# Gates of the linear recurrence: two products of 64 rows with both gates' columns, in place of two block-diagonal products of 128 rows

## The chip, the cores and the metric

The kernel runs on one core of one Trainium2 chip. A core has five engines with queues of their own: PE (TensorE, the matrix products; its weight loads are counted apart as PEld), DVE (VectorE), ACT (ScalarE), POOL (GpSimd) and SP (SyncE, which mainly issues DMAs). The time is that of one execution on the device in microseconds; the number that counts is the median of several executions.

## The reference, cut to what matters

One layer of a decoder trunk is computed for 2048 prompt tokens and 8 sample tokens. Each token's normed row goes through one input projection; a part of its columns feeds a retention block, another part a linear recurrence (RG-LRU), and both go through an output projection, a norm and a gated feed-forward part. The change touches the recurrence. Its 512 channels are 8 blocks of 64, and each block has two gates, `r` and `i`, with a 64x64 matrix each:

```python
xc, s_conv_lru_new = causal_dwconv(x_lru, s_conv_lru, conv_lru_w, conv_lru_b)
...
xb = x32.reshape(B, T, N_LRU_BLOCKS, LRU_BLOCK)
r = jax.nn.sigmoid(jnp.einsum('btnd,nde->btne', xb, w_r).reshape(B, T, W) + b_r)
i = jax.nn.sigmoid(jnp.einsum('btnd,nde->btne', xb, w_i).reshape(B, T, W) + b_i)
log_a = -LRU_C * r * jax.nn.softplus(-lam)
a = jnp.exp(log_a)
mult = jnp.sqrt(-jnp.expm1(2.0 * log_a))
...
bterm = mult * i * x32
# h[t] = a[t] * h[t-1] + bterm[t]
lru_out = hl * jax.nn.gelu(g_lru)
```

All inputs and outputs are 32-bit floats.

## The kernel before, in words

Channels lie on the 128 partitions and tokens run along the free dimension. The 2056 tokens are worked in three groups (0 to 2), one after the other; each group has two blocks of 336 to 344 tokens. The large products (input projection, output projection, feed-forward) are taken as three products in the type fp32r, of high and low parts, by the helper `mm3` (lines 371 to 375); a projection of one weight tile for one block (`proj`) is 8 times `mm3`, that is 24 products of 128x128 with up to 344 columns, into one of the three PSUM banks of the pool `pm`. Nearly everything that PE does is such products.

The recurrence's 512 channels are four tiles `t` of 128, two blocks of 64 in each. For one tile and one token block (24 such pairs in all) three pieces of code work:

- `lru_x` projects the tile's input. ACT copies the result from PSUM twice (lines 785 and 786: `xl`, and `xc` with the first term of the convolution), and the generator `lru_chain` is appended to the list `soon`.
- `lru_chain` adds three more terms of the convolution to `xc` on DVE (line 807), then yields. When it is resumed it takes two plain f32 products, `zr` and `zi` (lines 816 and 817), each with a 128x128 matrix that holds the tile's two 64x64 blocks on its diagonal and zeros elsewhere (`wri`, zeroed by POOL at line 241 and filled by four DMAs at line 246). One such f32 product stands in the trace as two matmul records. ACT evaluates `tanh` of both gates from PSUM (820, 822) and once more for the first gate (821); DVE, ACT and POOL make the decay, the gated input and the scan (823 to 834).
- `lru_g` projects the gate branch of the same tile and block, waits in the program's order until the chain is through (`while g.lru[t, b] is None: advance(soon)`), then ACT takes its GeLU from PSUM into `xc` (line 800) and DVE multiplies by the scan (801); `fsplit` (457, 458) splits the result into high and low parts `mlh` and `mll` for the output projection.

What sets the order: the program is traced item by item, and after each item of rate 1 `advance(soon)` resumes the first generator of `soon` up to its next yield (and goes on to the next generator if that one ends). For one tile `t` the items are `lru_x` of the first and second block, then `lru_g` of the first and second block. So a block's chain runs its convolution after its own `lru_x` or with the end of the other block's chain, and its products one item later. The order on each engine is then settled when the kernel is built: a scheduler simulates the program with a cost model and, among what is ready in that simulation, takes the earlier traced first. The queues then hold the instructions in the order that results. In each group, the items of tile 0 are followed by a head of the retention block (8 projections) and the first part of the output projection, those of tile 1 by another head and another part, and tiles 2 and 3 come one after the other, followed by the last head and the last parts.

PSUM: the pool `pm` has three banks (projections, output and down projections, some of the feed-forward's); the pool `pt` has five (`zr`, `zi`, the retention's tiles and others).

Of the kernel before, what the change touches and what calls it, by code (L numbers as in the profile page):

```python
# [13 lines left out]
AF = mybir.ActivationFunctionType  # L14
ALU = mybir.AluOpType

P = 128
# [81 lines left out]
def hybrid_step(ctx: ExitStack, tc: tile.TileContext, I, O):  # L99
    nc = tc.nc  # L100
    V, S, G, T = nc.vector, nc.scalar, nc.gpsimd, nc.tensor
# [12 lines left out]
    def ctile(cols, name, dt=F32):  # L114
        return con.tile([P, cols], dt, tag=name, name=name)

    def ttile(name):
        return tp.tile([P, BMAX + 4], F32, tag="t", name=name)
# [4 lines left out]
    def pst(name):  # L123
        return pt.tile([P, 512], F32, tag="t", name=name)
# [71 lines left out]
    clb, b_r, b_i = (vec[:, 64 + 4 * i:68 + 4 * i] for i in range(3))  # L196
# [10 lines left out]
    sp2, hbr, hbi = lc[:, 0:4], lc[:, 4:8], lc[:, 8:12]  # L207

    def lru_constants():
        V.tensor_scalar(out=hbr, in0=b_r, scalar1=0.5, scalar2=None, op0=ALU.mult)  # L210
        V.tensor_scalar(out=hbi, in0=b_i, scalar1=0.5, scalar2=None, op0=ALU.mult)
        y_ = tiny(4, "sp_y")
        V.tensor_scalar(out=y_, in0=lam, scalar1=-1.0, scalar2=None, op0=ALU.mult)
        V.tensor_tensor(out=y_, in0=y_, in1=lam, op=ALU.max)
        t_ = tiny(4, "sp_t")
        S.activation(out=t_, in_=y_, func=AF.Tanh, scale=1.0 / 32.0)
        d_ = tiny(4, "sp_d")
        V.tensor_scalar(out=d_, in0=t_, scalar1=1.0, scalar2=None, op0=ALU.add)
        V.reciprocal(d_, d_)
        V.tensor_scalar(out=t_, in0=t_, scalar1=-1.0, scalar2=1.0, op0=ALU.mult, op1=ALU.add)  # L220
        V.tensor_tensor(out=t_, in0=t_, in1=d_, op=ALU.mult)
        for _ in range(4):
            V.tensor_tensor(out=t_, in0=t_, in1=t_, op=ALU.mult)

        V.tensor_scalar(out=d_, in0=t_, scalar1=2.0, scalar2=None, op0=ALU.add)
        V.reciprocal(d_, d_)
        V.tensor_tensor(out=t_, in0=t_, in1=d_, op=ALU.mult)
        w2_ = tiny(4, "sp_w")
        V.tensor_tensor(out=w2_, in0=t_, in1=t_, op=ALU.mult)
        V.memset(d_, 1.0 / 17.0)  # L230
        for n in (15, 13, 11, 9, 7, 5, 3, 1):
            V.tensor_tensor(out=d_, in0=d_, in1=w2_, op=ALU.mult)
            V.tensor_scalar(out=d_, in0=d_, scalar1=1.0 / n, scalar2=None, op0=ALU.add)
        V.tensor_tensor(out=d_, in0=d_, in1=t_, op=ALU.mult)
        V.tensor_scalar(out=y_, in0=lam, scalar1=-1.0, scalar2=0.0, op0=ALU.mult, op1=ALU.max)
        V.scalar_tensor_tensor(out=y_, in0=d_, scalar=2.0, in1=y_, op0=ALU.mult, op1=ALU.add)
        V.tensor_scalar(out=sp2, in0=y_, scalar1=2.0, scalar2=None, op0=ALU.mult)


    wri = ctile(8 * P, "wri")  # L240
    G.memset(wri, 0.0)
    wriv = wri.rearrange("p (g t c) -> p g t c", g=2, t=4)
    for gi, nm in enumerate(("w_r", "w_i")):
        src = I[nm][0].rearrange("(t u) d e -> u d t e", u=2)
        for u in range(2):
            nc.gpsimd.dma_start(out=wriv[64 * u:64 * u + 64, gi, :, 64 * u:64 * u + 64], in_=src[u])
    for i in range(1, len(stage)):
        if i % 2:
            two = ttile("rows")
# [91 lines left out]
    def fetch_operand(key, lo_on):  # L341
# [25 lines left out]
        if (i == 1 or i == 2 and kind == "w_up_conv") and nm in ("A11", "A12"):  # L367

            del pr[nm]

    def mm3(out, wh, wl, xh, xl, first, last, more=False):

        T.matmul(out, wh, xh, start=first, stop=False, skip_group_check=more)  # L373
        T.matmul(out, wh, xl, start=False, stop=False, skip_group_check=more)  # L374
        T.matmul(out, wl, xh, start=False, stop=last, skip_group_check=more)  # L375

    ada_ps = {}

# [95 lines left out]
    class Group:  # L474
# [329 lines left out]
        def lru_chain(g, t, b, xl, xc):  # L804
            n, np_ = b[1] - b[0], g.npr(b)
            for j in range(3):
                V.scalar_tensor_tensor(out=xc[:, 0:np_], in0=xl[:, j:j + np_],
                                       scalar=clw[:, j, t:t + 1], in1=xc[:, 0:np_],
                                       op0=ALU.mult, op1=ALU.add)
                if np_ < n:  # L810
                    V.scalar_tensor_tensor(out=xc[:, np_:n], in0=slc[:, :, j, t],
                                           scalar=clw[:, j, t:t + 1], in1=xc[:, np_:n],
                                           op0=ALU.mult, op1=ALU.add)
            yield
            zr, zi = pst("zr"), pst("zi")
            T.matmul(zr[:, 0:n], wriv[:, 0, t, :], xc[:, 0:n], start=True, stop=True)
            T.matmul(zi[:, 0:n], wriv[:, 1, t, :], xc[:, 0:n], start=True, stop=True)
            s_, ti, rec = ttile("s"), ttile("ti")[:, 0:n], xl[:, 0:n]
            hs, s_ = s_, s_[:, 0:n]
            S.activation(out=s_, in_=zr[:, 0:n], func=AF.Tanh, scale=0.5, bias=hbr[:, t:t + 1])  # L820
            S.activation(out=s_, in_=s_, func=AF.Tanh, scale=sp2[:, t:t + 1], bias=sp2[:, t:t + 1])
            S.activation(out=ti, in_=zi[:, 0:n], func=AF.Tanh, scale=0.5, bias=hbi[:, t:t + 1])
            V.tensor_scalar(out=rec, in0=s_, scalar1=1.0, scalar2=None, op0=ALU.add)
            V.reciprocal(rec, rec)
            V.scalar_tensor_tensor(out=ti, in0=ti, scalar=1.0, in1=xc[:, 0:n], op0=ALU.add, op1=ALU.mult)
            S.activation(out=s_, in_=s_, func=AF.Sqrt)
            G.tensor_tensor(out=s_, in0=s_, in1=rec, op=ALU.mult)
            if g.gi == 0 and b[0] == 0:
                V.memset(s_[:, 0:1], 0.5)
            G.tensor_tensor(out=ti, in0=ti, in1=s_, op=ALU.mult)  # L830
            V.tensor_scalar(out=rec, in0=rec, scalar1=2.0, scalar2=-1.0, op0=ALU.mult, op1=ALU.add)
            V.tensor_tensor_scan(out=hs[:, 0:np_], data0=rec[:, 0:np_], data1=ti[:, 0:np_],
                                 initial=o_h[:, t:t + 1], op0=ALU.mult, op1=ALU.add)
            V.tensor_copy(o_h[:, t:t + 1], hs[:, np_ - 1:np_])
            if np_ < n:
                V.tensor_tensor(out=hs[:, np_:n], in0=rec[:, np_:n], in1=slh[:, :, t], op=ALU.mult)
                V.tensor_tensor(out=hs[:, np_:n], in0=hs[:, np_:n], in1=ti[:, np_:n], op=ALU.add)
                V.tensor_copy(o_hs[:, :, t], hs[:, np_:n])
            g.lru[t, b] = (hs[:, 0:n], xc[:, 0:n])
# [504 lines left out]
    for gi, g in enumerate(gs):  # L1344
        its = group_items(g, gs[gi + 1] if gi + 1 < len(gs) else None)
        if gi == 0:
            todo = [(j, k) for j in (2, 4, 3, 5) for k in range(KC)]
            mixed, c = [], 0.0
# [12 lines left out]
    g = gs[0]  # L1361
    xl = g.xload()

    more = [slot("more").rearrange("p a t -> p (a t)") for _ in range(7)]
    rest = [t[:, 2048:4 * TMAX] for t in more]
    more = [t[:, c:c + 1024] for t in more for c in (0, 1024)]
# [86 lines left out]
```

## Time and profile before

| | |
|---|---|
| median of 3 executions | 2462.89 us (2462.57 to 2464.89) |
| the profiled execution | 2463.86 us, of which 2462.1 us from its first to its last instruction |
| mean granted clock of TensorE | 0.988 |
| PE idle within the span | about 102 us |
| f32 gate products | 48, in 96 matmul records |

The profile counts an engine as busy from an instruction's start to its end. PE's instructions are pipelined: a product's recorded duration is longer than the distance to the next one, so what a product costs PE is read from the distances between starts. A line of the list of waits says which engine and line waited for which, then the sum in us, how often, and the longest. A line of the list of instruction groups has, after the count, the busy time and the mean duration in ns, then the idle time of the engine before these instructions and what ended it. In the windows view each row is a stretch of the span with the busy time of each engine, the granted clock and the DMA share.

### The profile page before, as it was taken

Reading aid. Unit: us, or ns where it says so; the run is one execution under the profiler, and the core shown is the slowest. Engines: PE = TensorE matmul, PEld = TensorE weight load, DVE = VectorE, ACT = ScalarE, POOL = GpSimd, SP = SyncE. Lnnn points to the kernel's source line nnn. Section 1 sums busy time; section 2 is a strip of 40 time slices with the busy share of each in tenths; the row PEclk is TensorE's granted clock in tenths of the full one; section 3 lists DMA queues with packets and bytes.
Section 4 is the critical chain, followed back from the end, with each engine's and each line's share of the span. In section 5 each row is a group of like instructions: output and inputs, shape, how many; then the busy total and the mean of one; then the engine's idle time right before and its main releaser. Section 6 shows DMA issues by size and latency. Waiting matters only on the chain.

```text
span 2462.1 us, 40114 instructions
## 1 busy us (share of the span) xinstructions
PE 2359.8 (96%) x15157; PEld 2275.5 (92%) x15157; DVE 1452.9 (59%) x3181; ACT 869.6 (35%) x1964; POOL 716.9 (29%) x739
## 2 busy tenths in 40 slices
PE   5999998999999999999899999999999989999998
PEld 4987797999999999999899999999999989999998
DVE  5646777875766665666754444446667675444444
ACT  4323554544444444243422222243124241222222
POOL 3444440257666743243001010112222210101011
PEclk9999999999999999999999999999999999999999
DMA  9476655878878875343566666666442465666674
GB/s 299 163 261 223 210 172 190 305 276 287 304 285 304 323 251 184 120 157 139 189 222 235 222 238 220 241 213 215 139 130 96 145 231 199 239 220 234 219 252 160
DMA packets 243493, 536.04 MB, mean 218 GB/s; under 512 B 19223, under 2 KB 114055, under 8 KB 243292
## 3 DMA queue, kind: packets, MB, share of 16 engines
q1 hardware_dynamic: 242220, 532.01, 62.6%
q8 instruction: 120, 1.97, 0.3%
q10 hardware_dynamic: 696, 0.91, 0.1%
q0 software_dynamic: 384, 0.56, 0.1%
q14 instruction: 73, 0.60, 0.1%
HBM read 385.10 MB, written 148.42 MB: 217 GB/s over the span
## 4 chain that ended last, share of the span: by engine, by line
PE 53%; DVE 4%; ACT 2%; DMA 1%; issue 1%; POOL 1%; POOLq 0%; SPq 0%; ACTq 0%; DVEq 0%
PE down L374 6%; PE down L373 6%; PE down L375 6%; PE qx L374 4%; PE qx L375 4%; PE qx L373 4%; PE proj L373 3%; PE proj L375 3%; PE proj L374 3%; PE qz L373 2%; PE qz L374 2%; PE qz L375 2%; PE qy L374 1%; PE qy L373 1%; PE qy L375 1%
## 5 line engine op out<-in xcount | busy, mean ns | idle before, releaser
L851 DVE SCALAR_TENSOR_TENSOR x<-down,mod,x 128x344 f32<-128x344 f32 (+2 forms) x624 | 349.0, 569 | 347.0 <-PE down L375 342.3
L373 PE MATMUL proj<-hh,wb 128*128 128x344 f32 (+1 forms) x1152 | 378.5, 329 | 14.3 <-DVE h L580 6.0
L375 PE MATMUL proj<-hh,wb 128*128 128x344 f32 (+1 forms) x1152 | 373.6, 325 | 2.7 <-POOL wb L304 2.5
L374 PE MATMUL proj<-hl,wb 128*128 128x344 f32 (+1 forms) x1152 | 372.5, 323 | 0.0
L458 POOL TENSOR_TENSOR ffl<-cv,ffh 128x344 fp32r<-128x344 f32 (+1 forms) x120 | 124.7, 1046 | 782.0 <-ACT ffh L457 736.7
L374 PE MATMUL qx<-op,wb 128*128 128x344 f32 (+1 forms) x1020 | 325.5, 319 | 2.6 <-DVE op L921 2.6
L373 PE MATMUL qx<-op,wb 128*128 128x344 f32 (+1 forms) x1020 | 324.7, 320 | 1.2 <-ACT op L920 1.2
L375 PE MATMUL qx<-op,wb 128*128 128x344 f32 (+1 forms) x1020 | 324.5, 319 | 0.0
L373 PE MATMUL down<-ffh,wb 128*128 128x344 f32 (+1 forms) x960 | 304.7, 324 | 7.6 <-DVE x L851 7.4
L375 PE MATMUL down<-ffh,wb 128*128 128x344 f32 (+1 forms) x960 | 306.4, 319 | 0.0
L374 PE MATMUL down<-ffl,wb 128*128 128x344 f32 (+1 forms) x960 | 306.3, 319 | 0.0
L304 POOL TENSOR_TENSOR wb<-wr,wb 128x512 fp32r<-128x512 f32 x164 | 223.9, 1376 | 230.7 <-ACT wb L303 222.1
L373 PEld LDWEIGHTS proj<-hh,wb 128*128 128x128 f32 x1152 | 218.4, 190 | 25.9 <-issue 9.5
L375 PEld LDWEIGHTS proj<-hh,wb 128*128 128x128 f32 x1152 | 218.7, 190 | 5.7 <-POOL wb L304 3.9
L374 PEld LDWEIGHTS proj<-hl,wb 128*128 128x128 f32 x1152 | 219.1, 190 | 3.3 <-POOL hl L588 0.9
L1076 DVE SCALAR_TENSOR_TENSOR cv<-u,vec,cv 128x344 f32<-128x344 f32 (+2 forms) x264 | 170.8, 665 | 50.6 <-ACT cv L1056 48.1
L374 PEld LDWEIGHTS qx<-op,wb 128*128 128x128 f32 x1020 | 191.7, 188 | 3.4 <-DVE op L921 3.4
L373 PEld LDWEIGHTS qx<-op,wb 128*128 128x128 f32 x1020 | 191.5, 188 | 2.0 <-ACT op L920 1.8
L373 PEld LDWEIGHTS down<-ffh,wb 128*128 128x128 f32 x960 | 179.3, 188 | 14.3 <-DVE x L851 13.7
L375 PEld LDWEIGHTS qx<-op,wb 128*128 128x128 f32 x1020 | 191.4, 188 | 0.0
L373 PE MATMUL qz<-op,wb 128*128 128x344 f32 (+1 forms) x528 | 169.7, 325 | 14.6 <-ACT op L920 10.7
L375 PEld LDWEIGHTS down<-ffh,wb 128*128 128x128 f32 x960 | 180.6, 188 | 0.0
(314 smaller groups left out, 4952.1 us busy)
## 6 DMA issues: line engine op xcount, KB each, us to landing
wb<-w_down SPq DMA_DIRECT2D x100, 512.0 KB
wb<-w_up_conv_S SPq DMA_DIRECT2D x92, 512.0 KB
wb<-w_up_gate_S SPq DMA_DIRECT2D x92, 512.0 KB
wb<-w_in SPq DMA_DIRECT2D x72, 512.0 KB
wb<-w_up_conv_A SPq DMA_DIRECT2D x69, 512.0 KB
wb<-w_up_gate_A SPq DMA_DIRECT2D x69, 512.0 KB
w_in<-wb SPq DMA_DIRECT2D x48, 512.0 KB
w_up_conv_S<-wb SPq DMA_DIRECT2D x44, 512.0 KB
```

The lines of the kernel that those rows point to most:

```text
L304: lo_on.tensor_tensor(out=w[:, 512:1024], in0=src, in1=w[:, 0:512].bitcast(F32), op=ALU.subtract)
L373: T.matmul(out, wh, xh, start=first, stop=False, skip_group_check=more)
L374: T.matmul(out, wh, xl, start=False, stop=False, skip_group_check=more)
L375: T.matmul(out, wl, xh, start=False, stop=last, skip_group_check=more)
L458: G.tensor_tensor(out=lo[:, 0:n], in0=src, in1=hi[:, 0:n].bitcast(F32), op=ALU.subtract)
L851: V.scalar_tensor_tensor(out=xs, in0=q[:, 0:np_], scalar=modv[:, jg, m, 0:1], in1=xs, op0=ALU.mult, op1=ALU.add)
L1076: V.scalar_tensor_tensor(out=cv[:, 0:np_], in0=u[:, j:j + np_], scalar=cfw[:, j, ft:ft + 1], in1=cv[:, 0:np_], op0=ALU.mult, op1=ALU.add)
```

## The change

The two 64x64 blocks of a tile are no longer put on the diagonal of one 128x128 matrix for each gate. Instead, each half of the partitions has one product: rows 0 to 63 of `xc` against 64x128 weights that hold both gates' columns of that block, and rows 64 to 127 likewise. The columns are placed so that the `r` gate of a block comes out on its own partitions and the `i` gate on the other half. ACT reads each gate in two halves from the two banks (the `i` gate's halves are moved to the other partitions by the same instruction), so there are five ACT instructions on the products where there were three. The bias of the `i` gate is stored with its halves swapped. `wri` has half the size, every element of it is written by the DMAs, and the memset goes.

Further, the chain yields once more before its products, and the two products are bound to come, in PE's queue, after the last `mm3` product traced so far (`tc.issue_after` adds an ordering edge without a semaphore). By the order of items above, the products of a chain are then traced within `lru_g` of the same tile and block, right after its projection.

```diff
-        V.tensor_scalar(out=hbi, in0=b_i, scalar1=0.5, scalar2=None, op0=ALU.mult)
+
+        for u in range(2):
+            V.tensor_scalar(out=hbi[64 * (1 - u):64 * (1 - u) + 64], in0=b_i[64 * u:64 * u + 64], scalar1=0.5,
+                            scalar2=None, op0=ALU.mult)
...
-    wri = ctile(8 * P, "wri")
-    G.memset(wri, 0.0)
-    wriv = wri.rearrange("p (g t c) -> p g t c", g=2, t=4)
+    wri = ctile(4 * P, "wri")
+    wriv = wri.rearrange("p (t c) -> p t c", t=4)
...
-            nc.gpsimd.dma_start(out=wriv[64 * u:64 * u + 64, gi, :, 64 * u:64 * u + 64], in_=src[u])
+            c = 64 * ((u + gi) % 2)
+            nc.gpsimd.dma_start(out=wriv[64 * u:64 * u + 64, :, c:c + 64], in_=src[u])
...
+    last_mm = [None]
...
-        T.matmul(out, wl, xh, start=False, stop=last, skip_group_check=more)
+        last_mm[0] = T.matmul(out, wl, xh, start=False, stop=last, skip_group_check=more)
...
             yield
-            zr, zi = pst("zr"), pst("zi")
-            T.matmul(zr[:, 0:n], wriv[:, 0, t, :], xc[:, 0:n], start=True, stop=True)
-            T.matmul(zi[:, 0:n], wriv[:, 1, t, :], xc[:, 0:n], start=True, stop=True)
+            yield
+
+            zs = [pst("z0"), pst("z1")]
+            halves = [slice(64 * u, 64 * u + 64) for u in range(2)]
+            with tc.issue_after(last_mm[0].ins):
+                for z, hf in zip(zs, halves):
+                    T.matmul(z[:, 0:n], wriv[hf, t, :], xc[hf, 0:n], start=True, stop=True)
...
-            S.activation(out=s_, in_=zr[:, 0:n], func=AF.Tanh, scale=0.5, bias=hbr[:, t:t + 1])
+            for z, hf in zip(zs, halves):
+                S.activation(out=s_[hf], in_=z[hf, 0:n], func=AF.Tanh, scale=0.5, bias=hbr[hf, t:t + 1])
             S.activation(out=s_, in_=s_, func=AF.Tanh, scale=sp2[:, t:t + 1], bias=sp2[:, t:t + 1])
-            S.activation(out=ti, in_=zi[:, 0:n], func=AF.Tanh, scale=0.5, bias=hbi[:, t:t + 1])
+            for z, hf, other in zip(zs, halves, halves[::-1]):
+                S.activation(out=ti[hf], in_=z[other, 0:n], func=AF.Tanh, scale=0.5, bias=hbi[other, t:t + 1])
```

## The prediction

> **What bounds the kernel now.** I read the page first, then the list of PE's waits, then PE's instruction groups.
>
> ```profile
> span 2462.1 us, 40114 instructions
> ...
> PE 2359.8 (96%) x15157; PEld 2275.5 (92%) x15157; DVE 1452.9 (59%) x3181; ACT 869.6 (35%) x1964; POOL 716.9 (29%) x739
> ```
>
> PE is busy for 2359.8 of 2462.1 us; 102 us are idle. So only two things shorten this kernel: fewer microseconds of product on PE, or fewer waits on PE. The other engines have room on average, and matter where PE waits for one of them.
>
> ```profile
> PE zr L816 <- DVE xc L807: 6.2, 3, 2.9
> ...
> PE proj L373 <- DVE rotb L624: 4.6, 3, 1.9
> ```
>
> ```profile
> L373 PE MATMUL down<-mlh,wb 128*128 128x344 f32 (+1 forms) x192 | 62.2, 324 | 0.0
> ...
> L816 PE MATMUL zr<-xc,wri 128*128 128x344 f32 (+1 forms) x48 | 19.3, 484 | 6.2 <-DVE xc L807 6.2
> L817 PE MATMUL zi<-xc,wri 128*128 128x344 f32 (+1 forms) x48 | 18.4, 467 | 0.0
> ```
>
> The reader is to see two costs of the gates: 96 records of product, and three waits of 6.2 us in sum for the convolution (line 807) just before `zr`. The output projection never waits for the recurrence's result `mlh` (0.0 idle), so a later chain has room at its far end.
>
> **The products.** Their cost is read from starts, in a quiet place of the timeline:
>
> ```profile
> 277.86 0.32 PE L373 MATMUL proj<-hh,wb 128*128 128x344 f32 x1
> 278.01 0.32 PE L374 MATMUL proj<-hl,wb 128*128 128x344 f32 x1
> 278.17 0.32 PE L375 MATMUL proj<-hh,wb 128*128 128x344 f32 x1
> 278.33 0.74 PE L816 MATMUL zr<-xc,wri 128*128 128x344 f32 x2
> 278.90 0.74 PE L817 MATMUL zi<-xc,wri 128*128 128x344 f32 x2
> 279.22 0.58 PE L373 MATMUL proj<-hh,wb 128*128 128x344 f32 x1
> 279.64 0.32 PE L374 MATMUL proj<-hl,wb 128*128 128x344 f32 x1
> ```
>
> A projection's product takes 0.157 us from start to start (277.86 to 278.33 hold three). From 278.17 to 279.64 are 1.47 us, with two such products in them; the four f32 records cost 1.47 - 0.31 = 1.156 us, 0.289 each. For 24 chains that is 27.7 us. After the change a chain still has four records of as many columns. They are cheaper only if the two halves of the array work side by side. No row shows two products on different rows. The nearest show products on different columns of the array (shape 128*2, on four separate strips), and what it costs to leave the full shape and come back:
>
> ```profile
> 1716.17 0.31 PE L374 MATMUL proj<-hl,wb 128*128 128x344 f32 x1
> 1716.41 0.48 PE L756 MATMUL os<-vts,sTs 8*128 8x128 f32 x2
> 1716.62 0.27 PE L756 MATMUL os<-vts,sTs 8*128 8x128 f32 x1
> 1716.82 0.29 PE L759 MATMUL os<-sret,qm 128*2 128x128 f32 x4
> ...
> 1716.83 0.61 PE L759 MATMUL os<-sret,qm 128*2 128x128 f32 x15
> 1717.37 0.42 PE L375 MATMUL proj<-hh,wb 128*128 128x344 f32 x1
> 1717.64 0.45 PE L816 MATMUL zr<-xc,wri 128*128 128x344 f32 x1
> ```
>
> Fifteen f32 records of 128 columns (0.107 us each by the rate above, 1.6 in a row) are done in 0.61 us; and four records of 0.27 us stand within 0.29, so they start within 0.02. Products on separate column strips do run together. I take the same for row halves: 2 x 0.289 + 0.01 = 0.59 us for the pair.
>
> Against it stands the change of shape. From line 374 to the 8-row product of line 756 pass 0.24 us, 0.08 more than 0.157. Its second record comes 0.21 later, where 128 columns take 0.107 at the rate above: 0.10 more, a weight load that nothing hides. On the way back the last record starts at 1716.83 + 0.61 - 0.27 = 1717.17 and should end its columns at 1717.28; the projection's product starts at 1717.37, 0.09 late, and the next at +0.27 in place of 0.157, 0.11 late. An excursion costs 0.08 + 0.10 + 0.09 + 0.11, some 0.39 us with the roundings. So a chain takes 0.59 + 0.39 = 0.98 in place of 1.156: **24 x -0.18 = -4.3 us**. Bounds: nothing for the excursion gives 24 x -0.57 = -13.6; halves one after the other give 24 x 0.39 = +9.4; if the two halves' first loads follow each other (0.10 more) it is -1.9. I take -4.3, the sum of the nearest rows.
>
> The Trainium skill, "TensorEngine Tiling (Array Packing)", section Overview, gives up to 2x for a contract dimension of 64 or less; by that alone the streaming would shrink by half, which is the -13.6. The same page, Tiling Modes, says that changing the mode drains TensorE, without a figure; the 0.39 us of the rows is what it takes here, and two thirds of the gain go there.
>
> **The waits before the products.** The windows around the two longest:
>
> ```profile
> 298.64:301.48 2.84, 0.32 (x2) 0.02 (x2) 2.80 (x5) 1.72 (x3) 1.94 (x2) 1.00 0.58 186
> 302.90:306.40 3.50, 3.50 (x12) 2.12 (x10) 2.97 (x5) 2.17 (x6) 1.27 (x1) 0.51 0.89 277
> 1105.61:1108.50 2.89, 0.31 (x3) 0.03 (x1) 2.85 (x7) 0.77 (x3) 1.31 (x2) 1.00 0.34 135
> 1108.50:1111.90 3.40, 3.06 (x7) 2.14 (x8) 3.33 (x5) 2.03 (x5) 2.55 (x2) 0.50 0.41 117
> 266.00:312.00 46.00, 41.27 (x241) 33.33 (x240) 36.15 (x45) 28.72 (x48) 20.91 (x18) 0.96 0.64 193
> ```
>
> In the first and third row PE stands while DVE (third busy column) works without a break. In the second and fourth the granted clock is half: the PE work there, 3.50 and 3.06 us, would take half the time, a loss of 1.7 + 1.5 = 3.2 us. The half clock follows each of the two long waits, so I charge it to them: 6.2 + 3.2 = **9.4 us**. With the change the products stand one projection later, 24 x 0.157 = 3.77 us, and the longest wait was 2.9. These three waits should go: **-9.4**. All lie in the stretch of tiles 2 and 3, where chains follow each other closely.
>
> **What comes in their place.** The chain now ends one item later, so its DVE and ACT work reaches further into the retention head that follows. In such heads PE already waits for DVE's rotation, 4.6 us in three waits (the list above), 1.5 us each. I charge three more, one per group, behind its last chains: **+4.6**. Bounds: nothing, since `mlh` has a head of eight projections (30 us) before it is read; and above, the bank rival below.
>
> ACT has two instructions more per chain:
>
> ```profile
> L826 ACT ACT_TABLE_LOAD x24 | 30.8, 1283 | 0.4
> L800 ACT ACT_TABLE_LOAD x19 | 24.4, 1283 | 1.3 <-DVE s L829 0.9
> L821 ACT ACTIVATE s<-s,lc 128x344 f32<-128x344 f32 (+1 forms) x24 | 16.1, 669 | 0.1
> ...
> L820 ACT ACTIVATE s<-zr,lc 128x344 f32<-128x344 f32 (+1 forms) x24 | 13.0, 542 | 18.1 <-PE zr L816 18.1
> L822 ACT ACTIVATE ti<-zi,lc 128x344 f32<-128x344 f32 (+1 forms) x24 | 13.0, 540 | 1.0 <-PE zi L817 0.6
> L826 ACT ACTIVATE s<-s 128x344 f32<-128x344 f32 (+1 forms) x24 | 11.8, 490 | 0.3
> L800 ACT ACTIVATE xc<-proj 128x344 f32<-128x344 f32 (+1 forms) x24 | 10.9, 456 | 0.4
> ```
>
> A half of the partitions has as many columns, so I take 0.54 us for each half: 48 x 0.54 = 26 us of ACT. In the tightest window (266 to 312) that is 4 x 1.08 = 4.3 us on 28.7 of 46: hidden by PE's own work. If a half could take half the time, ACT would gain nothing and lose nothing; PE would not notice. The chain's latency grows by 1.1 us.
>
> At the start POOL's one memset goes; PE's first products wait for loads on SP's queue, not on POOL's: 0, either way less than the spread of the executions. The second half of `hbi` is one more DVE instruction of 4 columns beside the same loads: 0. The products take no new semaphore; behind them in PE's queue stands the next projection, and it would wait with them.
>
> **Sum.** -4.3 - 9.4 + 4.6 = -9.1 us. Against the profiled execution, 2463.86 - 9.1 = 2454.8; this execution is 1.0 above the median of 2462.89, so the forecast is **2453.8 us**.
>
> **The rivals.**
>
> *Late GeLU holds PSUM (slower).* `lru_g`'s bank is free only after line 800, which now waits for the chain: products 0.98, ACT 2 x 0.542 + 0.669 + 2 x 0.540, root with its table load 1.283 + 0.490, GeLU 1.283 + 0.456, together 7.3 us. Its bank comes round after the products and two more projections, 0.98 + 2 x 3.77 = 8.5. Slack: 1.2 us. ACT's queue shows what eats it:
>
> ```profile
> ACT mlh L457 <- DVE xc L801: 43.2, 18, 5.7
> ```
>
> ACT stands 2.4 us on average, 18 times, at the split of the former chain. If PE met each of these beyond the slack, it would lose 18 x 1.2 = 21.7 us: -4.3 - 9.4 + 21.7 = +8.0, 2470.9. It decides from an ACT delay of 1.2 us. For it: ACT's order is fixed. Against: the scheduler can put the split behind the copies, and the windows leave ACT a third idle. Chance 0.13.
>
> *The halves run one after the other* (the change doesn't do what it says): +9.4 - 9.4 + 4.6 = +4.6, 2467.5. For it: no row shows row halves side by side. Against: columns do. Chance 0.10.
>
> *Strict order of records.* If a half's second record has to end before the other half's first begins to overlap, three record times remain: 3 x 0.289 + 0.01 + 0.39 = 1.27, 24 x +0.11 = +2.7; in sum -2.1, 2460.8. The Trainium skill, "TensorE: Matmul & The Clock Gate", Part 3, states that matmuls start and end in strict program order, which would be this case; the four records of line 759 above, each the first of its product's two, start ahead of the seconds, which speaks against it. Chance 0.07.
>
> *The waits come back elsewhere.* DVE is busy 36 of 46 us in the tightest window; if PE meets the same 9.4 us at another place, only -4.3 remain: 2458.6. Chance 0.10.
>
> *No price for the change of shape:* -13.6 - 9.4 + 4.6 = -18.4, 2444.5. Against it stand the rows of line 756. Chance 0.08.
>
> **How the numbers follow.** The forecast keeps 0.52. What a measurement can tell from no change is about 0.2%, 4.9 us: faster is below 2458.0, slower above 2467.8. Faster: 0.46 of the forecast, the free change of shape 0.08, 0.04 of the waits elsewhere, 0.58. Slower: 0.11 of the bank rival and 0.04 of the serial halves, 0.15. Same: 0.27. The range leaves out the free change of shape and the bank rival (0.20 or so): from the forecast without new waits, 2449.2, less the spread of the three executions (2.3), to the serial halves: 2446.9 to 2468.
>
> **What would show it.** The two products' first records start within 0.02 us of each other and the pair takes 0.59; the product after them starts 0.1 late and the next 0.1 late. The line "PE zr <- DVE xc" is gone, and the half clock near 303 and 1108 with it. ACT is busier by 26 us. Wrong if starts lie 0.58 us apart between the halves, or if PE waits for ACT's line 800 before a projection.

## The result and the profile after

The changed kernel takes 2491.14 us (median of 4, 2489.39 to 2493.89), the kernel before 2462.73 us beside it (median of 4, 2459.01 to 2464.89): **28.4 us slower**, a ratio of 1.0128 with a 95% interval of 1.0107 to 1.0149. The forecast was 2453.8 us and the range ended at 2468. In the table of runs below, one execution of e4 (2888.16 us, granted clock 0.748) and one of e17 (2590.35 us, 0.844) ran in a slower state of the chip and are left out.

The page of the changed kernel, its span and its busy time by engine:

```profile
span 2489.4 us, 40169 instructions
...
PE 2366.1 (95%) x15157; PEld 2276.1 (91%) x15157; DVE 1441.5 (58%) x3182; ACT 924.4 (37%) x2031; POOL 716.4 (29%) x738
```

PE is busy 6 us longer, and 123 us of the span are idle where it was 102. ACT is busy 54.8 us longer (869.6 to 924.4).

First the products themselves, in the timeline of PE after (start, duration, line, tiles):

```profile
1098.40 0.32 PE L380 MATMUL proj<-hh,wb 128*128 128x340 f32 x1
1098.65 0.84 PE L826 MATMUL z<-xc,wri 64*128 64x340 f32 x4
1099.42 0.42 PE L378 MATMUL proj<-hh,wb 128*128 128x340 f32 x1
1099.68 0.32 PE L379 MATMUL proj<-hl,wb 128*128 128x340 f32 x1
```

From 1098.40 to 1099.68 are 1.28 us with two projection records of 0.157 in them; the four records of the gates cost 0.97 us, where 0.98 was forecast. Read the same way, the six chains that stand between two projections, without a wait, cost 0.97 to 0.98 us. The halves run side by side, as the starts of single records in the trace show at another chain:

```
start us   ns   what
1028.645  317   L380 proj 128*128
1028.892  550   L826 z 64*128
1028.899  550   L826 z 64*128
1029.282  446   L826 z 64*128
1029.289  446   L826 z 64*128
```

In a later run (e1) some halves stand alone in PE's queue: the two records of one half then start 0.39 us apart, so of the four records here the first two, 7 ns apart, are of different halves. A half alone costs 0.96 to 0.97 us there, as much as both together here. So the change does on PE what it says. The time is lost in PE's waits. The list of PE's waits after:

```profile
PE proj L378 <- ACT xc L805: 16.9, 7, 4.7
...
PE z L826 <- DVE xc L812: 4.8, 1, 4.8
```

Before, there was no line for a projection that waits for the GeLU (now line 805). It is now the longest of the list, seven waits of 16.9 us. The wait for the convolution is one in place of three, but it takes 4.8 us where the three took 6.2.

One of these waits from both sides, first ACT's timeline, then PE's:

```profile
1896.65 0.49 ACT L462 ACTIVATE mrh<-head 128x344 fp32r<-128x344 f32 x1 [10.19 <-DVE head L680]
1897.15 0.54 ACT L830 ACTIVATE s<-z,lc 64x344 f32<-64x344 f32 x1
...
1901.81 0.54 ACT L833 ACTIVATE ti<-z,lc 64x344 f32<-64x344 f32 x1
1902.37 1.28 ACT L805 ACT_TABLE_LOAD   x1
1903.67 0.46 ACT L805 ACTIVATE xc<-proj 128x344 f32<-128x344 f32 x1
```

```profile
1899.14 0.32 PE L380 MATMUL proj<-hh,wb 128*128 128x344 f32 x1
1904.18 0.42 PE L378 MATMUL proj<-hh,wb 128*128 128x344 f32 x1 [4.71 <-ACT xc L805]
```

ACT has waited 10.19 us for a retention head, with the tanhs of two blocks behind that instruction in its queue; PE had taken the products of both blocks only just before, from 1896.27 on. Then eight halves of 0.54 us, a second tanh, and a table load pass before the GeLU reads its PSUM bank, and PE's next projection waits 4.71 us for the bank. A stretch of about half clock follows both of these stops, as it followed the two long ones before. The windows behind the wait of 4.8 us and behind this one (the granted clock is the figure after POOL's: 0.50 and 0.57):

```profile
1122.30:1126.00 3.70, 3.63 (x12) 2.70 (x13) 2.72 (x7) 3.03 (x5) 1.26 (x1) 0.50 0.28 113
...
1904.00:1908.00 4.00, 3.82 (x14) 3.83 (x15) 1.05 (x3) 3.95 (x6) 1.04 (x2) 0.57 0.02 4
```

**Where ACT's 54.8 us come from.** ACT's instruction groups after (count, busy us, mean ns):

```profile
L837 ACT ACT_TABLE_LOAD x24 | 30.8, 1283 | 0.4
L805 ACT ACT_TABLE_LOAD x22 | 28.2, 1283 | 0.4
L833 ACT ACTIVATE ti<-z,lc 64x344 f32<-64x344 f32 (+1 forms) x48 | 26.0, 542 | 1.0
L830 ACT ACTIVATE s<-z,lc 64x344 f32<-64x344 f32 (+1 forms) x48 | 26.0, 542 | 23.9 <-PE z L826 23.1
L830 ACT ACT_TABLE_LOAD x14 | 18.0, 1283 | 0.6 <-PE z L826 0.3
L634 ACT ACT_TABLE_LOAD x9 | 11.5, 1283 | 0.2
L1096 ACT ACT_TABLE_LOAD x3 | 3.8, 1283 | 0.1
```

A half takes 0.542 us, as the whole did: 52.0 us in place of 26.0, as forecast. Not forecast are the table loads: with two single ones there are 74, where the kernel before had 55. Nineteen more are 24.4 us. Together that is 50.4 of the 54.8 us.

The chain of waits shows what that does. It is read backwards from the last instruction; the stretch is that of tiles 2 and 3 of the second group. Before (start, us, what), then after:

```profile
1095.39 0.67 ACT s L821
1096.06 0.45 ACT wb L303
1096.59 1.28 ACT L826
1097.89 0.49 ACT s L826
1098.39 1.28 ACT L800
1099.69 0.45 ACT xc L800
```

```profile
1103.47 0.79 ACT L805
1104.27 0.46 ACT xc L805
1104.75 1.28 ACT L837
1106.04 0.49 ACT s L837
1106.53 0.52 ACT wb L306
1107.07 1.28 ACT L830
1108.36 0.54 ACT s L830
1108.91 0.54 ACT ti L833
1109.48 0.54 ACT s L830
1110.05 0.55 ACT ti L833
1110.61 0.67 ACT s L831
1111.30 1.28 ACT L805
1112.70 0.37 issue
1113.07 1.28 ACT L837
1114.36 0.49 ACT s L837
```

A line without a tile is a table load. Before, ACT leads for some 5 us, with two loads. After, it leads for 11 us with no break to speak of, with five loads: GeLU's, the root's, one for the next block's tanhs, and GeLU's and the root's again. PE's wait of 4.8 us, which begins at 1117, comes behind this stretch, for DVE's work that it held up.

This stretch is an example of the order of loads, and not the place where most of the time is lost. In the traces' records, the part of a group from its first projection to its first feed-forward product took 355.2, 299.4 and 306.3 us before, and with the change 17.9 us more in the first group, 0.4 less in the second and 16.2 more in the third. (One profiled execution each. In e7, whose queues hold the order of the kernel before, the same parts differ by up to 3.0 us.)

### The profile page after: what moved, and what is told of

Read it like the earlier page. It is cut to its first block, busy times and chain, and to the rows that moved or that the text cites. A ratio compares the mean times of both kernels' runs of the same rounds, so it can differ in the third digit from the quotient of the medians.

```text
span 2489.4 us, 40169 instructions
## 1 busy us (share of the span) xinstructions
PE 2366.1 (95%) x15157; PEld 2276.1 (91%) x15157; DVE 1441.5 (58%) x3182; ACT 924.4 (37%) x2031; POOL 716.4 (29%) x738
## 4 chain that ended last, share of the span: by engine, by line
PE 55%; DVE 5%; ACT 3%; DMA 1%; issue 1%; POOL 1%; POOLq 0%; SPq 0%; DVEq 0%; ACTq 0%
PE down L379 6%; PE down L380 6%; PE down L378 6%; PE qx L379 4%; PE qx L380 4%; PE qx L378 4%; PE proj L378 4%; PE proj L380 4%; PE proj L379 4%; PE qz L378 2%; PE qz L379 2%; PE qz L380 2%; PE qy L378 1%; PE qy L379 1%; PE qy L380 1%
## 5 line engine op out<-in xcount | busy, mean ns | idle before, releaser
L378 PE MATMUL proj<-hh,wb 128*128 128x344 f32 (+1 forms) x1152 | 385.2, 335 | 30.0 <-ACT xc L805 16.9
L380 PE MATMUL proj<-hh,wb 128*128 128x344 f32 (+1 forms) x1152 | 378.6, 329 | 1.4 <-POOL wb L307 1.4
L379 PE MATMUL proj<-hl,wb 128*128 128x344 f32 (+1 forms) x1152 | 379.4, 329 | 0.0
L380 PE MATMUL down<-ffh,wb 128*128 128x344 f32 (+1 forms) x960 | 306.3, 319 | 0.2 <-POOL wb L307 0.2
L378 PEld LDWEIGHTS proj<-hh,wb 128*128 128x128 f32 x1152 | 224.9, 195 | 43.6 <-ACT xc L805 18.9
L380 PEld LDWEIGHTS proj<-hh,wb 128*128 128x128 f32 x1152 | 224.6, 195 | 4.9 <-POOL wb L307 2.6
L379 PEld LDWEIGHTS proj<-hl,wb 128*128 128x128 f32 x1152 | 225.0, 195 | 4.0 <-issue 2.9
L379 PEld LDWEIGHTS down<-ffl,wb 128*128 128x128 f32 x960 | 180.6, 188 | 0.0
```

Source lines behind the costliest of these rows:

```text
L380: last_mm[0] = T.matmul(out, wl, xh, start=False, stop=last, skip_group_check=more)
```

## The experiments

Four theories stood at the start. **A:** the late place, which makes the GeLU hold its PSUM bank. **B:** ACT's additional instructions, as load on ACT or as time on the chain's path. **C:** luck of the order that the scheduler gives. **D:** products of 64 rows that cost PE more than the records show. A later one is **T:** table loads. All runs are set against runs of the kernel before on the same chip.

| run | median us | less that of before | ratio, 95% interval |
|---|---|---|---|
| e1 halves, old place | 2485.35 | +23.7 | 1.0093 [1.0078, 1.0107] |
| e2 128 rows, new place | 2467.84 | +6.2 | 1.0027 [1.0018, 1.0035] |
| e3 changed, GeLU into its own tile | 2482.04 | +20.4 | 1.0080 [1.0066, 1.0095] |
| e4 changed, not pinned | 2489.91 | +28.3 | 1.0122 [1.0100, 1.0144] |
| e5 before, both gates read in halves | 2486.30 | +25.5 | 1.0093 [1.0079, 1.0108] |
| e6 changed, three ACT instructions | 2469.09 | +8.3 | 1.0034 [1.0022, 1.0046] |
| e7 before, bias in two parts | 2459.92 | -0.9 | 0.9999 [0.9989, 1.0009] |
| e8 before, memset on DVE | 2458.11 | -2.7 | 0.9985 [0.9976, 0.9994] |
| e9 before, first gate in halves | 2468.71 | +8.6 | 1.0037 [1.0025, 1.0050] |
| e10 before, second gate in halves | 2466.97 | +6.8 | 1.0026 [1.0017, 1.0036] |
| e11 before, 48 more ACT copies off the chain | 2463.81 | +3.7 | 1.0019 [1.0010, 1.0028] |
| e12 before, no root | 2443.04 | -17.1 | 0.9936 [0.9924, 0.9947] |
| e13 halves, no root | 2448.78 | -12.1 | 0.9950 [0.9933, 0.9966] |
| e14 changed, no root | 2454.93 | -6.0 | 0.9977 [0.9965, 0.9988] |
| e15 before, paired roots | 2462.37 | +1.5 | 1.0009 [0.9997, 1.0022] |
| e16 e15, GeLU into its own tile | 2466.64 | +5.8 | 1.0024 [1.0014, 1.0034] |
| e17 before, table loaded early | 2461.76 | +0.9 | 1.0008 [0.9998, 1.0019] |
| e18 changed, table loaded early | 2477.34 | +16.5 | 1.0067 [1.0052, 1.0082] |

### Place or halves: e1 and e2

e1 is the changed kernel without the second yield and the pin; e2 is the kernel before with both.

```diff
 e1, on the changed kernel
-            yield
...
-            with tc.issue_after(last_mm[0].ins):
-                for z, hf in zip(zs, halves):
-                    T.matmul(z[:, 0:n], ...)
+            for z, hf in zip(zs, halves):
+                T.matmul(z[:, 0:n], ...)
 e2, on the kernel before
+            yield
...
+            with tc.issue_after(last_mm[0].ins):
+                T.matmul(zr[:, 0:n], wriv[:, 0, t, :], xc[:, 0:n], start=True, stop=True)
+                T.matmul(zi[:, 0:n], wriv[:, 1, t, :], xc[:, 0:n], start=True, stop=True)
```

> The two 64-row products as in the change, at the chain's old place: one yield, no pin behind the last projection. Theory A (the later place of the chain costs, since the GeLU waits for the chain and holds a PSUM bank): the waits for the GeLU line are under 3 us, the pairs of products still take 0.97 us each, and the time is 2453 to 2463 us (2462.7 less the 4.3 us of the products, give or take the 5 us by which a new order moves it). Rival B (the additional ACT instructions, 26 us, and table loads lengthen the chain wherever it stands): 2470 to 2490 us, with ACT named in PE's longest waits.

> The old products of 128 rows, but with the additional yield and the pin behind the last projection: the movement alone. Theory A: slower like the changed kernel, 2485 to 2500 us (2491.1 plus the 4.3 us of the products), with PE waiting for the GeLU line 10 us or more. Rival B: 2455 to 2468 us, since ACT has no instruction more than before.

The place alone costs 6.2 us; everything else without the place costs 23.7. So the larger part lies in what e1 kept. In e1 the scheduler pulled the two halves of 5 of the 24 chains apart; each of these ten halves stands alone, at 0.96 to 0.97 us where it was read between two projections. e1 met the price of B, e2 only just (2467.84 against an end of 2468).

### The bank and the pin: e3 and e4

```diff
 e3, on the changed kernel
+            gl = fp.tile([P, BMAX], F32, tag="f", name="gl")[:, 0:n]
+            S.activation(out=gl, in_=q, func=AF.Gelu_apprx_tanh)
...
-            S.activation(out=xc, in_=q, func=AF.Gelu_apprx_tanh)
-            V.tensor_tensor(out=xc, in0=xc, in1=hs, op=ALU.mult)
+            V.tensor_tensor(out=xc, in0=gl, in1=hs, op=ALU.mult)
 e4, on the changed kernel: the products without tc.issue_after
```

> The changed kernel, but the GeLU goes to a tile of its own, ahead of the wait for the chain, so that a projection's bank is free as soon as ACT comes to it. Theory A: the 16.9 us of PE waiting for the GeLU are gone and with them some of the half clock: 2460 to 2475 us. Rival B: 2480 us or more, the waits move to other ACT lines. If it were the order in general that costs (Rival C, waits spread over many lines), also 2480 us or more, with no ACT line over 4 us.

> The changed kernel without the pin: the additional yield stays, and the scheduler is free to put the two products where it likes. Theory A (the place in the traced order decides, not the pin): within 6 us of 2491. If the pin itself did the harm: 2455 to 2470 us.

In e3 the GeLU no longer needs the recurrence. The list of its PE waits has now

```profile
PE proj L378 <- DVE rotb L629: 14.7, 4, 6.9
...
PE proj L378 <- ACT gl L803: 5.8, 4, 3.4
```

The 16.9 us on the bank fall to 5.8, and 14.7 us on the retention's rotation, DVE's work as well, take their place (3.4 in the changed kernel). The time is that of Rival B, though the waits moved to DVE and not to other lines of ACT. The bank is one place where PE meets the late chain, not the whole cause; and part of the 8 to 9 us that e3 gains over the changed kernel need not be the bank's, for its trace has 49 table loads, not 74. e4: the pin costs nothing that can be measured.

### ACT's instructions: e5 to e8

```diff
 e5, on the kernel before (products and places untouched)
-            S.activation(out=s_, in_=zr[:, 0:n], func=AF.Tanh, scale=0.5, bias=hbr[:, t:t + 1])
+            for hf in halves:
+                S.activation(out=s_[hf], in_=zr[hf, 0:n], func=AF.Tanh, scale=0.5, bias=hbr[hf, t:t + 1])
...
 likewise ti
 e6, on the changed kernel: one instruction for each bank
+            S.activation(out=s_, in_=zs[0][:, 0:n], func=AF.Tanh, scale=0.5, bias=hbr[:, t:t + 1])
+            S.activation(out=ti, in_=zs[1][:, 0:n], func=AF.Tanh, scale=0.5, bias=hbi[:, t:t + 1])
 e7: hbi in two instructions    e8: V.memset(wri, 0.0) in place of G.memset
```

> The kernel before with its two products of 128 rows, but with each gate read from PSUM by ACT in two halves (48 ACT instructions more, as in the change). Theory B (the additional ACT instructions cost wherever the chain stands): 2475 to 2490 us. Theory C (the halves cost little by themselves; each build gives the queues a new order, and the one before was a good one): anywhere from 2458 to 2485 us, with PE's lost time spread over several lines, none of them the ACT lines of the gates. Theory D (the 64-row products cost on PE): 2458 to 2468 us.

> The changed kernel, but each of the two banks is read by ACT in one instruction over all 128 partitions, so that the gates of the odd blocks are exchanged and ACT has no instruction more than before. Theory B: the 28 us go away, 2455 to 2470 us. Theory D: it stays at 2480 us or more, with the products' places as the cause. Theory C: between 2455 and 2485, and what PE waits for differs from the changed kernel at many places.

> The kernel before with one small instruction more: the bias of the second gate is halved in two parts of 64 partitions (0.16 us of DVE at the start, which nothing waits for). Theories B and D: no change, 2458 to 2466 us. Theory C: the new order of the queues alone may move it by 5 us or more, either way.

> The kernel before with the memset of the gate weights on DVE in place of POOL, nothing else: about 1 us of work at the start changes engines. Theories B and D: no change beyond 2 us, 2458 to 2466 us. Theory C: the new order of the queues alone may move it by 5 us or more, either way.

The kernel before with nothing but the halved ACT instructions loses 25.5 us, nearly all that the change loses. The changed kernel with three ACT instructions in place of five keeps 8.3 (its gates of the odd blocks are exchanged, so its output is not the reference's). DVE's wait for ACT's `ti`, in the lists of DVE's waits of before, of the changed kernel and of e5:

```profile
DVE ti L825 <- ACT ti L822: 22.8, 16, 3.2
```

```profile
DVE ti L836 <- ACT ti L833: 40.1, 20, 5.5
```

```profile
DVE ti L828 <- ACT ti L825: 46.3, 17, 5.5
```

In e6 this line is back at 21.3 us. What stands behind `ti` in DVE's queue, the retention's work among it, waits with it. The line is no measure of the loss by itself: in e10 below it is 6.2 us, and PE waits 10.6 us for the GeLU instead.

C is not tested by e7 and e8. In e7 the queues of PE, ACT and POOL hold the order of the kernel before, instruction for instruction, so its -0.9 us shows how well two builds agree. e8 has another order at the start and in the first group's feed-forward part (350 to 650 us), and almost none in the recurrence; it is 2.7 us faster. In e5 itself the halves came with another order: 641 of PE's records, all in the parts of the groups ahead of the feed-forward, stand elsewhere in its queue, ACT has four table loads more (59), and from the second tanh of one block to that of the next pass 7.2 us in the mean in place of 5.4, of which two more halves are 1.1. What speaks against luck is that the builds agree: the five with the halves of both gates and the root (e1, e3, e4, e5, the change) lose 20 to 28 us, the two with whole instructions at the new place (e2, e6) 6 and 8. How much of the 25.5 us is the halves' own time and how much the order that came with them, no run separates.

D falls: halves for whole rows, with ACT's instructions kept the same in number, is e5 to e1 (-1.8 us) and e2 to e6 (+2.1), about nothing either way.

### On the chain or off it: e9 to e12

```diff
 e9: only s_ in halves          e10: only ti in halves
 e11, on the kernel before, behind line 802
+            for _ in range(2):
+                S.activation(out=g.mixt[4 + t][b][0], in_=xc, func=AF.Copy)
 e12, on the kernel before
-            S.activation(out=s_, in_=s_, func=AF.Sqrt)
```

> The kernel before with only the first gate read in halves (24 ACT instructions more, 13 us of ACT). Theory L (load: in the stages of the recurrence a microsecond of ACT is worth about a microsecond of PE, wherever it stands): 2468 to 2478 us, half of what both gates' halves cost. Theory P (path: the later end of the second tanh delays DVE's reciprocal, and with it the retention's normalisation that stands behind it in DVE's queue): 2478 to 2488 us, nearly all of it.

> The kernel before with only the second gate read in halves (24 ACT instructions more, 13 us of ACT). Theory L: 2468 to 2478 us. Theory P: ACT takes the second gate ahead of the second tanh, so it delays that as well: then as much as the first gate's halves; if the scheduler puts it behind, 2458 to 2466 us.

> The kernel before with 48 useless ACT instructions that nothing in the chain waits for: the high part of the recurrence's result is copied twice more after its low part is made (48 x 0.48 = 23 us of ACT). The output projection reads it some 30 us later. Theory L: 2475 to 2490 us, as for both gates' halves. Theory P: 2458 to 2468 us.

> The kernel before without the square root of the recurrence (24 ACT instructions of 0.49 us and most of 43 table loads of 1.28 us are left out, some 60 us of ACT; the output is not the reference's). Both theories, if ACT in these stages is what costs: faster, 2435 to 2452 us. If ACT is slack in the kernel before and only a surplus costs: 2455 to 2462 us.

Forty-eight more instructions off the chain raise ACT's busy time from 869.6 to 890.4 and cost 3.7 us; as many on it (e5) cost 25.5. So it is for the most part the path, not the load. Without the root and its table loads (53 of the 55) 17.1 us go, as both theories had it: ACT's part of the chain had been holding up the kernel before already. DVE's wait for `ti` in e12, against 22.8 before:

```profile
DVE ti L825 <- ACT ti L822: 8.8, 7, 1.8
```

The halves of each gate alone cost 8.6 and 6.8 us, the two together 25.5: more than the sum, as where slack is used up. Taken alone, e9 and e10 did not bear P out: e9 lies at the low end of L's range and 9 us below P's, and e10 just above what P gave for halves behind the second tanh, where the scheduler put one or both of them in 21 of the 24 chains. It is e11 that decides, by 11 us below L's range.

### The halves without the root: e13 and e14

e13 is e5 and e14 the changed kernel, each without the root.

> The kernel before with ScalarE reading each of the two gates in two halves of 64 partitions, and with the square root left out (so no table load for it; the output is not the reference's). If ScalarE's time between products and scan is what costs, the root and its loads leave room in that loop and the halves cost little here: 2443 us of the run without the root plus 4 to 8, so 2447 to 2451, with VectorE's wait for the second gate near 10 to 20 us. If the halves cost by themselves, wherever the loop stands (a bank held longer, another order): 2443 + 25, so about 2468.

> The changed kernel with the square root left out (the output is not the reference's). If ScalarE's loop is the cause, the change costs 0 to 10 us over the kernel before without its root, 2440 to 2453. If the late place of the products or the products themselves cost, 28 us over it: about 2471.

With the root gone, the same halves cost 5.7 us (2448.78 against 2443.04 of e12; 5.0 by the losses against the kernel before on each chip) in place of 25.5, within what was expected. The whole change costs 11.9 (11.1 by the losses) in place of 28.4, a little more than the 10 that were expected at most. So the halves cost little by themselves, and the more the fuller the path is to which they add. The rest of e14 (6.1 us over e13) is as large as the late place in e2.

### Table loads: e15 to e18

```diff
 e15, on the kernel before: what follows line 825 is put off until both blocks are so far
+            both.append((s_, rest))
+            if len(both) == 2:
+                for v, _ in both:
+                    S.activation(out=v, in_=v, func=AF.Sqrt)
+                for _, fn in both:
+                    fn()
 e16: e15, and the GeLU into its own tile as in e3
 e17 on the kernel before, e18 on the changed one
-            S.activation(out=s_, in_=s_, func=AF.Sqrt)
+            root = S.activation(out=s_, in_=s_, func=AF.Sqrt)
+            with tc.issue_after(root.ins):
+                S.activation(out=sink, in_=hbr[:, t:t + 1], func=AF.Gelu_apprx_tanh)
```

> The kernel before; the roots of a tile's two token blocks are taken one behind the other, when the second block's chain has come so far, so that some 24 of ScalarE's table loads of 1.28 us go (about 31 us of ScalarE). If ScalarE's time in the loop counts, 2448 to 2458 us. If the delay of the first block's root counts more (its scan, and with it the GeLU that waits for it, come 5 us later), 2463 to 2480, with PE's wait for line 800's GeLU grown.

> As the run with paired roots, and the GeLU writes a tile of its own ahead of its wait for the recurrence, so that PSUM is let go of early. If the bank that waits for the GeLU is what paired roots cost, this gives 2445 to 2456 us. If own tiles move waits to the rotation's chain, as in the changed kernel, 2456 to 2470.

> The kernel before with one more ScalarE instruction per chain, a GeLU of one constant column pinned behind the root. It brings the table with GeLU and tanh back at once: 49 table loads in place of 55, none of them between a GeLU and the root any more. If each us of ScalarE in the loop costs about 0.8 us of the span, as the halves did (25.5 us of span for 31 us of halves and loads), 6 x 1.28 x 0.8 = 6 us less, 2455. If table loads are hidden: 2461, or 1 to 2 more for 24 instructions.

> The changed kernel with the same instruction. Its page shows 74 table loads where the kernel before has 55: with the products late, the next block's tanhs come between root and GeLU, and tanh, GeLU and root each bring a load. Pinned, 50 remain. If these loads are what the late place costs and the halves cost the rest, the 6 us of the late place go: about 2485. If every us of ScalarE in the loop counts alike, 24 x 1.28 x 0.8 = 25 us go: about 2466, as much as the kernel before or little above. If loads are hidden and the order alone costs: 2491.

e15 didn't test what it was made for: its trace has the same 55 table loads, for the roots came out apart in ACT's order all the same. e16 has 50, as the GeLU there may go ahead, and is 4 us slower than e15; what its own tile costs isn't told apart from what five loads give. Neither of e15's ranges was met, and neither run decides on T.

e18 does. A GeLU of one column behind each root brings the table back at once, and 74 loads become 50: 12 to 14 us come back (the loss falls from 28.4 to 16.5, the median from 2491.14 to 2477.34). ACT's timeline in e18 for two blocks:

```profile
1032.32 0.67 ACT L833 ACTIVATE s<-s,lc 128x340 f32<-128x340 f32 x1
1032.90 0.43 ACT L807 ACTIVATE xc<-proj 128x340 f32<-128x340 f32 x1
1033.35 1.28 ACT L839 ACT_TABLE_LOAD   x1
1034.64 0.49 ACT L839 ACTIVATE s<-s 128x340 f32<-128x340 f32 x1
1035.15 1.28 ACT L841 ACT_TABLE_LOAD   x1
1036.44 0.20 ACT L841 ACTIVATE sink<-lc 128x1 f32<-128x1 f32 x1
1036.55 0.53 ACT L832 ACTIVATE s<-z,lc 64x340 f32<-64x340 f32 x1
...
1038.80 0.67 ACT L833 ACTIVATE s<-s,lc 128x340 f32<-128x340 f32 x1
```

From the second tanh of one block to that of the next pass 6.5 us here. By the same reading it was 5.1 us before (1018.24 to 1023.37) and 7.8 in the changed kernel (1032.01 to 1039.83); the means of the twelve pairs of blocks are 7.4, 5.4 and 8.4. In the kernel before, six loads fewer (e17, 49) show no gain; it has 24 small instructions more, and on the path that is read below it stands at 10.1 us against 10.2.

None of the three expectations of e18 was met: 6 us would have been the late place's alone, 25 us every load at full price, and nothing at all if loads were hidden. A little under half of the loss is the 24 loads, with the halves beside them; the other part (e18 less e17, 15.6 us) is the halves and the place. The parts do not add up one by one: the late place with its 18 loads more (e2 has 73) costs 6.2 us with whole ACT instructions, while beside the halves 24 loads fewer give some 12.

### The path, read across the runs

From the traces' records: the mean time from the start of ACT's copy that starts the convolution (`xc`, line 786 of the kernel before) to the start of the second tanh of the gate (821), for the second block of each of the twelve pairs. The runs without the root are not in the table, since the root lies behind the second tanh.

| products' place | run: us on this path, loss |
|---|---|
| old | before 10.2, 0; e11 10.3, +3.7; e10 10.6, +6.8; e9 11.7, +8.6; e5 13.5, +25.5; e1 13.8, +23.7 |
| late (3.8 us by design) | e6 14.1, +8.3; e2 14.1, +6.2; e3 15.4, +20.4; e18 16.0, +16.5; e4 17.1, +28.3; the change 17.1, +28.4 |

Within each place the loss grows with the path, but not evenly: e5 and e1 stand out of order, as do e3 and e18. Some 3 us on the path, twelve times, go with 20 to 25 us of the span. The two rows do not lie on one line; in the late place 3.8 us of the path pass, by design, while PE works on the projection that was put ahead.

## Why the prediction was wrong, point by point

**The products: right, and worth little.** Side by side, 0.97 us a chain for 0.98, next product late by its share; the rivals of serial halves and of strict order fall. The Trainium skill, "TensorE: Matmul & The Clock Gate", Part 3, has matmuls start and end in program order; in the records above the other half's first record starts 7 ns after the first's and ahead of the first's second record. In which order the four records stand in the program the trace does not show, so the rival falls, but the rule is not refuted. The 4.3 us are real on PE. They are not seen at the end (e1 against e5, e6 against e2), where the chain sets the time.

**ACT's instructions: the step that failed.** The prediction costed them at nothing: "hidden by PE's own work". It set 26 us of ACT, or 4.3 us in the tightest window, against ACT's idle share there. That reading took ACT's idle time for room. In those stretches ACT's idle time stands before the chain (18.1 us in sum at line 820) and behind it (43.2 us at the split, line 457), and once the products are done its tanhs, root and loads follow each other without a gap to speak of (before, from 1017.17 to 1027.62, ACT stands nowhere for more than 0.1 us); DVE and the GeLU's bank wait for them. The measured price: e5 puts the halves, with the order that came with them, at 25.5 us, where the prediction had 0. e11 shows that a like load on ACT off the chain costs 3.7.

**ACT's size: off by half.** 54.8 us more, not 26. The prediction's own rows showed 24 loads for the root and 19 for the GeLU, but it took their number as given. The late place put the next block's tanhs between a root and a GeLU, and that order needs three loads where root, GeLU, tanh needs two. The Trainium skill, "ScalarE: Activation LUTs", section Table sets, names tanh in two sets, that of exp and that of sigmoid, and says of the set of gelu that `gelu_apprx_tanh`, the function of this kernel, is separate from it; which set holds it is not said. It advises to batch calls by set. The 19 more loads agree with the advice, and e18 shows that the table loaded for this GeLU serves tanh as well.

**The three waits before the products: half right.** The extra projection does hide the convolution where it comes in time, and two of the three waits go. But the chain before it ends so much later that one wait of 4.8 us at 1117 replaces them, with its half clock, and others arise where there were none. That one wait is not the halves' alone: with whole ACT instructions at the new place it is 4.6 us (e2) and 5.0 (e6).

**What comes in their place: the term was there, its size was not.** Three waits for the rotation were charged, 4.6 us. In the changed kernel they are 3.4 in sum, one fewer than before. What came is the rival *Late GeLU holds PSUM*, by its own mechanism (seven waits, 16.9 us, an ACT delay far beyond the 1.2 us of slack), with chance 0.13. But it had only ACT's order in view, and the halves only as a term of 7.3 us; the result lies 20 us beyond its price, and with the bank's waits cut from 16.9 to 5.8 us (e3) 20.4 of the loss were left.

**`hbi` and the memset: right for `hbi`** (e7, -0.9 us, no change). The memset moved to DVE (e8) gives 2.7 us, with another order in the first feed-forward part.

No version of the products was found that beats the kernel before. Of all runs with the whole computation only e8 is faster, by 0.15%, and its products are the old ones.

What stays open: why the halves of both gates cost 10 us more than the sum of each (a queue that has used up its slack would do that, and e13 fits, but no run shows the threshold); how much of e5's 25.5 us is the order that the scheduler chose with the halves; and how the remaining loss of e18 divides between halves and place.

## What to carry to other kernels

An engine at 35% can still be the path: before an instruction is costed at zero, follow the chain that it lies on to whoever waits at its end, and look whether the engine is idle *within* that chain or only between two of them. Where a change moves work past other work on ACT, count the table loads that the new order needs; one tiny activation pinned behind the odd function can bring the common table back (12 us in e18, nothing in e17). And an operand read in two halves of the partitions costs ACT two instructions at the full price of each, 0.54 us here.

## What the runs showed of the hardware

- An ACT instruction on 64 partitions takes as long as on 128: 0.542 us in the mean over blocks of 340 and 344 columns, both.
- Two f32 products on the two row halves of the array start 7 ns apart and run together, and one alone takes PE as long (0.96 to 0.97 us in e1); leaving the full shape and coming back costs 0.39 us, as for the narrow products in the trace of before: 0.97 us for the four records, less 2 x 0.29.
- Each table load takes 1.28 us and the function starts 0.01 to 0.02 us behind it. The Trainium skill, "ScalarE: Activation LUTs", What ACT_TABLE_LOAD costs, gives 1283 ns too, and a drain of 1380 ns besides; no such drain stands in these rows (1033.35 + 1.28, the root at 1034.64, with the GeLU before it begun at 1032.90).
- Which table is loaded depends on the function that comes first: behind a root, a tanh brings one that does not hold this GeLU (in the changed kernel 14 loads stand at the tanhs and 22 more at the GeLU), a GeLU brings one that holds both (in e18 24 loads at the pinned GeLU, one at line 807's and none at the tanhs). The same activations in another order took 49 loads (e3) to 74 (the change).
